# Pools of transposed x, split weights and raw weights placed first in SBUF, their tiles at multiples of 512 bytes; descriptor scratch 8 KB

## The chip, the cores and the metric

The kernel runs on one core of one Trainium2 chip. The metric is the device time of one execution in microseconds. The time before is the median of three runs.

## The reference, cut to what matters

Two blocks of two layers each act on one sequence of 256 tokens of width 1024, all in float32.

```python
# first block, per layer: mixer (attention variants), then a mixture of 16 experts
x = x + mixer(rmsnorm(x))                   # projections in, attention, projection out
x = x + ec_moe(rmsnorm(x))                  # each expert takes its 32 best tokens; silu(g) * u, down
# second block, per layer: dense ffn, mixer, dense ffn
h = h + 0.5 * swiglu(rmsnorm(h), wg, wu, wd)      # 1024 -> 2816 -> 1024
h = h + mixer(rmsnorm(h))                          # attention + convolution, or a recurrence
h = h + 0.5 * swiglu(rmsnorm(h), wg, wu, wd)
return rmsnorm(h)
```

## The kernel before, in words

The order of the work is the order of the code: the first block's even mixer (`even1`), a mixture of experts (`moe`), the odd mixer (`odd1`), a second `moe`, then in the second block `ffn`, `even2`, `ffn`, `ffn`, `odd2`, `ffn`. SyncE (SP) issues nearly all loads, in program order, on one queue.

All projections of the mixers and of the dense ffn layers work on float32 operands that are split in two parts, hi and lo, of type fp32r. `xT` writes the normed and transposed x as two tiles, `hThi` and `hTlo` (pool `hT`, 8 KB per partition each). A raw weight lands in one of six 8 KB tiles of the pool `ring`. `split` casts 1024 columns of it into a `whi` tile on ScalarE and subtracts on VectorE into a `wlo` tile (pool `wsp`, seven of each, 4 KB each). One product is then three matmuls:

```python
    def mm3(self, out, a, b, start, stop):
        mm = self.nc.tensor.matmul
        mm(out, a[0], b[0], start=start, stop=False)
        mm(out, a[0], b[1], start=False, stop=False)
        mm(out, a[1], b[0], start=False, stop=stop)
```

These are lines L406, L407 and L408. The second argument is the operand that is loaded into the array (128 columns, 512 bytes of a partition), the third one streams past it. Three uses matter here:

- Up products of the ffn (`bg`, `bu`) and the projections in of the second block (`pf`): a piece of whi or wlo is loaded, 256 columns of hThi or hTlo stream.
- Token projections of the first block (`pj`): a piece of hThi or hTlo is loaded, 512 or 256 columns of whi or wlo stream.
- Down products of the ffn and projections out (`acc`): a piece of the activations is loaded (`gh`, `gl` in the ffn's pool `fp`; `chi`, `clo` in a mixer's own pool), 512 columns of whi or wlo stream.

In an ffn layer, each of 11 steps does 96 up matmuls and the 24 down matmuls of the step before.

The `moe` stages stream expert weights that are not split: 32 loads of gate and up (two of 1 MB each) and 32 of down, into whatever is free: the ring, pairs of whi and wlo tiles (4 KB each), the two hT tiles, and up to eight extra 8 KB tiles of the pools `moew...`.

Pools take their places in SBUF in the order in which they are opened, from low to high. The DMA descriptor scratch comes first (16 KB per partition by default). In the program as built, the tiles stand at these bytes of a partition; the number behind the stroke is the remainder by 512:

| tiles | before | with the change |
|---|---|---|
| hThi, hTlo | 26560, 34752 / 448 | 8704, 16896 / 0 |
| wlo and whi, 14 tiles of 4096 | from 46240 / 160 | from 25088 / 0 |
| ring, 6 tiles of 8192 | from 103584 / 160 | from 82432 / 0 |
| x | 16512 / 128 | 131584 / 0 |
| chi, clo of even1 and odd1 | 153248, 161440 / 160 | 145440, 153632 / 32 |
| gh, gl of the first ffn; of the other three | 288; 192 | 160; 64 |
| chi, clo of even2; of odd2 | 192; 256 | 64; 128 |
| moew tiles on the right side; the others | 480; 192 | 480; 64 |

Pieces inside hT, whi, wlo, chi, clo, gh and gl start at further multiples of 512 bytes, so each piece has its tile's remainder, but for the 416, 384 and 256 column blocks of a few projections in `odd1` and `even1`.

Of the kernel before, what the change touches and what calls it, by code (L numbers as in the profile page):

```python
# [9 lines left out]
F32 = mybir.dt.float32  # L10
# [6 lines left out]
P = 128  # L17
# [10 lines left out]
RING = 6  # L28
CHUNK = 2048
PART = 1024  # L30
WB = 7
TAPS = 11
LATER = 2000
PLAN = "7ssslhrrrrrr012ssss3456" "7ssslhrrrrrrssss456"
AHEAD = 23

# [189 lines left out]
class OddLead:  # L226


    def __init__(self, A):
        self.A = A  # L230
# [53 lines left out]
class Core:  # L284
    def __init__(self, ctx, tc, A, where):
        self.tc, self.nc, self.A, self.where = tc, tc.nc, A, where
        e = ctx.enter_context
        self.cst = e(tc.tile_pool(name="cst", bufs=1))
        self.hp = e(tc.tile_pool(name="hT", bufs=1))
        self.wk = e(tc.tile_pool(name="wk", bufs=2))  # L290
        self.jk = e(tc.tile_pool(name="jk", bufs=1))
        self.ps = e(tc.tile_pool(name="ps", bufs=8, space=PSUM))
        self.n = 0
        nc = self.nc
        self.tabs = {}
        self.x = self.cst.tile([P, NT, D], F32, name="x")
        self.small("id", self.cst, nc.sync)
        self.mhalf = self.cst.tile([P, 16], F32, name="mhalf")
        nc.vector.memset(self.mhalf, -0.5)
        self.id = self.c("ident")  # L300

    def pools(self, cx, ring, parts):

        self.wp = cx.enter_context(self.tc.tile_pool(name="wsp", bufs=parts, reuse_waits="tile"))
        self.ring = cx.enter_context(self.tc.tile_pool(name="ring", bufs=ring, reuse_waits="tile"))

    def begin(self):

# [809 lines left out]
    def early(self, names):  # L1118

        for n in names:  # L1120
            self.fetch(next(i for i in range(AHEAD) if PLAN[i] == n and i not in self.got))

# [3 lines left out]
    def at(self, i):  # L1126
        return PLAN[i] if i < len(PLAN) else "r"

# [390 lines left out]
    def even2(self, nxt):  # L1519
        nc, tc, A = self.nc, self.tc, self.A  # L1520
        with ExitStack() as cx:
# [20 lines left out]
            def taps(c):  # L1542

                b = self.bank("cv")
                for j in range(31 - TAPS, 31):
                    d = pl.tile([P, P], F32, name="dgc", bufs=8)
                    nc.gpsimd.tensor_scalar(d, self.id, cw[:, c, j:j + 1], None, op0=ALU.mult)
                    nc.tensor.matmul(b[:, :S], d, glu[:, c, j:j + S], start=j == 31 - TAPS, stop=j == 30)
                with tc.high_priority(-LATER):
                    nc.vector.tensor_tensor(y[:, c], y[:, c], b[:, :S], ALU.add)  # L1550
# [14 lines left out]
            def use(i, b):  # L1565
# [15 lines left out]
                nc.vector.tensor_tensor(glu[:, c, 30:], b, sg[:, c], ALU.mult)  # L1581
                with tc.high_priority(-LATER):
                    nc.vector.tensor_scalar(y[:, c], glu[:, c, :S], cw[:, c, 0:1], cb[:, c:c + 1], op0=ALU.mult,
# [184 lines left out]
def build(tc, A, out, where):  # L1768
    with ExitStack() as ctx:
        k = Core(ctx, tc, A, where)  # L1770
        k.want(k.c("g_mix0"))
        with ExitStack() as cx:
            k.pools(cx, RING, WB)
            leads = OddLead(A), FfnLead(A)
            k.even1(k.begin(), leads[0])
            gf0 = k.cst.tile([P, KT], F32, name="gf0")
            tc.nc.vector.tensor_tensor(gf0, k.c("g_fin"), k.c("g2_f0"), ALU.mult)
            k.moe(0, (k.c("g_mix1"),), leads[0])
            k.odd1(*leads)
            k.moe(1, (gf0,), leads[1])  # L1780
            pl = cx.enter_context(tc.tile_pool(name="c2", bufs=1, reuse_waits="tile"))
            pr = cx.enter_context(tc.tile_pool(name="c2r", bufs=1, side="right", reuse_waits="tile"))
            with tc.tile_pool(name="t5", bufs=1, reuse_waits="tile") as p5:
                k.ffn(0, leads[1], (k.c("g2_m0"),), hook=k.t5_bias(pl, p5))
            k.even2((k.c("g2_f1"),))
            k.ffn(1, None, (k.c("g2_f2"),))
            k.ffn(2, None, (k.c("g2_m1"),), hook=k.log_a(pr))
            k.odd2((k.c("g2_f3"),))
            k.ffn(3, out=out)
# [17 lines left out]
```

## Time and profile before

| | |
|---|---|
| median of 3 runs (range) | 1619.71 us (1617.31 to 1621.27) |
| the profiled execution's own time | 1622.63 us |
| its span | 1620.9 us |
| TensorE busy | 1471.1 us, 91% |
| VectorE, ScalarE, GpSimd busy | 840.8, 649.4, 114.2 us |
| moved by DMA | 398.68 MB |

The span is what the profiler saw of the program's instructions; the execution's own time is 1.7 us longer. A busy time is the union of an engine's instructions.

### The profile page before, as it was taken

The page shows a single profiled execution, that of the slowest core. Times are in us where ns is not written, and L with a number is a line of the kernel's source. Part 1 is how long each engine was busy: PE and PEld are TensorE (multiplying, and loading weights), DVE is VectorE, ACT ScalarE, POOL GpSimd, SP SyncE. Part 2 cuts the span into 40 slices and gives each one's busy share as a digit, 9 for nine tenths or more (in the row PEclk, how much of TensorE's full clock was granted, in tenths as well). Part 3 has the DMA queues.
Part 4 walks back from the last instruction along what each step waited for, and adds up shares of the span by engine and source line. Part 5 has one row for each costly group of instructions (what it writes and reads, how often), then busy time and mean ns, then how long its engine had stood idle before and what let it go on. Part 6 is the DMA issues. An engine that isn't in the chain of part 4 may idle for free.

```text
span 1620.9 us, 24647 instructions
## 1 busy us (share of the span) xinstructions
PE 1471.1 (91%) x10184; PEld 1163.8 (72%) x10184; DVE 840.8 (52%) x1418; ACT 649.4 (40%) x1035; POOL 114.2 (7%) x147
## 2 busy tenths in 40 slices
PE   9998867877988677799999799999999999999998
PEld 7784204555742045599898579999999999899997
DVE  6753102258421012555569966555666559865554
ACT  5741101137311012344443544444554446754443
POOL 0000000020000001200006610000000000000000
PEclk9998979998989799899999899999999999999999
DMA  9778999992799999856454125555555553555530
GB/s 361 305 261 344 418 422 419 413 379 107 264 384 418 422 414 382 343 186 222 164 177 157 52 81 195 192 183 185 180 184 188 194 188 131 196 193 196 184 130 27
DMA packets 60625, 398.68 MB, mean 246 GB/s; under 512 B 6808, under 2 KB 7200, under 8 KB 17120
## 3 DMA queue, kind: packets, MB, share of 16 engines
q1 hardware_dynamic: 59584, 394.03, 64.3%
q0 software_dynamic: 928, 3.07, 0.6%
q8 instruction: 80, 1.31, 0.3%
q14 instruction: 33, 0.27, 0.0%
HBM read 396.01 MB, written 1.06 MB: 245 GB/s over the span
## 4 chain that ended last, share of the span: by engine, by line
PE 74%; DMA 11%; DVE 10%; ACT 4%; issue 2%; SPq 0%; POOL 0%; POOLq 0%; DVEq 0%; ACTq 0%
PE acc L406 7%; PE acc L408 7%; PE acc L407 7%; DMA w<-in_m_gu_dram 6%; PE bg L407 5%; PE bg L406 5%; PE bg L408 5%; PE bu L407 5%; PE bu L408 5%; PE bu L406 5%; DMA w<-in_m_d_dram 3%; PE by L1297 3%; DVE y L1586 3%; PE bu L1243 3%; PE bg L1243 2%; PE xs L1226 2%
## 5 line engine op out<-in xcount | busy, mean ns | idle before, releaser
L395 DVE TENSOR_TENSOR wlo<-w,whi 128x1024 fp32r<-128x1024 f32 x346 | 424.2, 1234 | 277.0 <-ACT whi L394 276.7
L394 ACT CAST whi<-w 128x1024 fp32r<-128x1024 f32 (+1 forms) x357 | 370.3, 1046 | 440.1 <-PE acc L408 143.7
L406 PE MATMUL bg<-hThi,whi 128*128 128x256 f32 x752 | 211.7, 283 | 2.8 <-ACT hThi L452 2.3
L407 PE MATMUL bg<-hTlo,whi 128*128 128x256 f32 x752 | 210.5, 281 | 3.8 <-DVE hTlo L453 3.7
L408 PE MATMUL bg<-hThi,wlo 128*128 128x256 f32 x752 | 210.6, 280 | 0.0
L407 PE MATMUL bu<-hTlo,whi 128*128 128x256 f32 x656 | 183.7, 280 | 0.0
L406 PE MATMUL bu<-hThi,whi 128*128 128x256 f32 x656 | 183.7, 280 | 0.0
L408 PE MATMUL bu<-hThi,wlo 128*128 128x256 f32 x656 | 183.6, 280 | 0.0
L407 PEld LDWEIGHTS bg<-hTlo,whi 128*128 128x128 f32 x752 | 141.8, 189 | 7.4 <-DVE hTlo L453 5.6
L406 PEld LDWEIGHTS bg<-hThi,whi 128*128 128x128 f32 x752 | 141.7, 189 | 7.0 <-ACT hThi L452 3.9
L406 PE MATMUL acc<-whi,gh 128*128 128x512 f32 x352 | 140.2, 398 | 4.9 <-ACT gh L401 4.9
L408 PEld LDWEIGHTS bg<-hThi,wlo 128*128 128x128 f32 x752 | 142.0, 189 | 0.0
L408 PE MATMUL acc<-whi,gl 128*128 128x512 f32 x352 | 140.3, 399 | 0.0
L407 PE MATMUL acc<-wlo,gh 128*128 128x512 f32 x352 | 140.3, 398 | 0.0
L406 PEld LDWEIGHTS bu<-hThi,whi 128*128 128x128 f32 x656 | 124.0, 189 | 0.0
L407 PEld LDWEIGHTS bu<-hTlo,whi 128*128 128x128 f32 x656 | 124.0, 189 | 0.0
L408 PEld LDWEIGHTS bu<-hThi,wlo 128*128 128x128 f32 x656 | 123.9, 189 | 0.0
L406 PEld LDWEIGHTS acc<-whi,gh 128*128 128x128 f32 x352 | 66.7, 189 | 19.2 <-ACT gh L401 5.1
L408 PEld LDWEIGHTS acc<-whi,gl 128*128 128x128 f32 x352 | 66.7, 189 | 16.2 <-DVE gl L402 0.6
L407 PEld LDWEIGHTS acc<-wlo,gh 128*128 128x128 f32 x352 | 66.8, 190 | 14.1
L1297 PE MATMUL by<-w,aT 128*32 128x256 f32 x1024 | 67.7, 391 | 10.0 <-DMA w<-in_m_d_dram 6.9
L1276 DVE SCALAR_TENSOR_TENSOR hid<-bu,rsl,hid 128x512 f32<-128x512 f32 x8 | 6.0, 751 | 127.4 <-PE bu L1243 119.3
(402 smaller groups left out, 2374.7 us busy)
## 6 DMA issues: line engine op xcount, KB each, us to landing
w<-in_f_gu_dram SPq DMA_DIRECT2D x84, 1024.0 KB, 5.1
w<-in_m_gu_dram SPq DMA_DIRECT2D x68, 1024.0 KB, 13.7
w<-in_m_d_dram SPq DMA_DIRECT2D x64, 1024.0 KB, 10.9
w<-in_f_d_dram SPq DMA_DIRECT2D x40, 1024.0 KB, 5.0
wx<-in_m_gu_dram SPq DMA_DIRECT2D x32, 1024.0 KB, 9.4
wx<-in_m_gu_dram SPq DMA_DIRECT2D x56, 512.0 KB, 7.0
w<-in_e_out_dram SPq DMA_DIRECT2D x8, 1024.0 KB, 4.9
w<-in_o_out_dram SPq DMA_DIRECT2D x8, 1024.0 KB, 5.1
```

Of the source, the lines that this page charges most:

```text
L394: pin(nc.scalar.copy(hi[:, i:n], w[:, o + i:o + n]))
L395: pin((eng or nc.vector).tensor_sub(lo[:, i:n], w[:, o + i:o + n], hi[:, i:n].bitcast(F32)))
L406: mm(out, a[0], b[0], start=start, stop=False)
L407: mm(out, a[0], b[1], start=False, stop=False)
L408: mm(out, a[1], b[0], start=False, stop=stop)
L1226: nc.tensor.matmul(b[:, :n], self.x[:, t, k * P:k * P + P], ohf[:, t, q0 * P:q1 * P], start=t == 0, stop=t == NT - 1)
L1243: nc.tensor.matmul(b[32 * j:32 * j + 32], xs[q][:, k, 32 * j:32 * j + 32], w[j // 2][:, j % 2 * 512:j % 2 * 512 + 512], start=k == 0, stop ...
L1276: nc.vector.scalar_tensor_tensor(a, bu, rsl[:, q:q + 1], a, op0=ALU.mult, op1=ALU.mult)
L1297: nc.tensor.matmul(b[32 * j:32 * j + 32, o:o + S], aT[:, q, f, 32 * j:32 * j + 32], w[i][:, j * S:j * S + S], start=f == 0, stop=f == 3)
L1586: nc.vector.scalar_tensor_tensor(y[:, c], glu[:, c, j:j + S], cw[:, c, j:j + 1], y[:, c], op0=ALU.mult, op1=ALU.add)
```

## The change

It opens the pools `hT`, `wsp` and `ring` first, ahead of the constants. A new pool `line` of 384 bytes (512 less the 128 that the first free byte is past a multiple) brings them to a multiple of 512; its only tile is set to zero once. The descriptor scratch goes from 16 KB to 8 KB. All tiles keep their sizes and numbers of buffers.

```diff
+LINE = 512
+SCRATCH = 8192
...
         e = ctx.enter_context
+
+        self.line(e, 128)
+        self.hp = e(tc.tile_pool(name="hT", bufs=1))
+        self.wp = e(tc.tile_pool(name="wsp", bufs=WB, reuse_waits="tile"))
+        self.ring = e(tc.tile_pool(name="ring", bufs=RING, reuse_waits="tile"))
         self.cst = e(tc.tile_pool(name="cst", bufs=1))
-        self.hp = e(tc.tile_pool(name="hT", bufs=1))
         self.wk = e(tc.tile_pool(name="wk", bufs=2))
...
-    def pools(self, cx, ring, parts):
-
-        self.wp = cx.enter_context(self.tc.tile_pool(name="wsp", bufs=parts, reuse_waits="tile"))
-        self.ring = cx.enter_context(self.tc.tile_pool(name="ring", bufs=ring, reuse_waits="tile"))
+    def line(self, e, past):
+
+        pool = e(self.tc.tile_pool(name="line", bufs=1))
+        self.tc.nc.vector.memset(pool.tile([P, (LINE - past) // 4], F32, name="line"), 0.0)
...
         with ExitStack() as cx:
-            k.pools(cx, RING, WB)
...
-    nc = _bacc.Bacc("TRN2", target_bir_lowering=False, num_devices=1)
+    nc = _bacc.Bacc("TRN2", target_bir_lowering=False, num_devices=1, dynamic_dma_scratch_size=SCRATCH)
```

The order of instructions is the same on every engine but for one new row on VectorE. Its first rows before:

```order
L299 MEMSET mhalf 128x16
L327 MEMSET warm 128x512
L499 SCALAR_TENSOR_TENSOR junk,ss<-x 128x512 x2
L453 SCALAR_TENSOR_TENSOR hTlo<-tp,pc_id,hThi 128x256 x2
L395 TENSOR_TENSOR wlo<-wz,whi 128x512
```

With the change (lines are six further down):

```order
L311 MEMSET line 128x96
L305 MEMSET mhalf 128x16
L333 MEMSET warm 128x512
L505 SCALAR_TENSOR_TENSOR junk,ss<-x 128x512 x2
L459 SCALAR_TENSOR_TENSOR hTlo<-tp,pc_id,hThi 128x256 x2
L401 TENSOR_TENSOR wlo<-wz,whi 128x512
```

The new memset of 96 columns stands ahead of the two that were first; nothing else moved.

## Rows read from the trace of the kernel before

**Rows 1.** The page: span, busy time of engines, chain that ended last by engine.
```profile
span 1620.9 us, 24647 instructions
PE 1471.1 (91%) x10184; PEld 1163.8 (72%) x10184; DVE 840.8 (52%) x1418; ACT 649.4 (40%) x1035; POOL 114.2 (7%) x147
PE 74%; DMA 11%; DVE 10%; ACT 4%; issue 2%; SPq 0%; POOL 0%; POOLq 0%; DVEq 0%; ACTq 0%
```
**Rows 2.** Stages: window, length, busy PE PEld DVE ACT POOL, clock, DMA share, GB/s.
```profile
93.10:108.40 15.30, 15.30 (x69) 12.65 (x69) 9.87 (x34) 8.86 (x22) 0.00 (x0) 1.00 0.88 338
...
185.00:340.00 155.00, 114.84 (x942) 52.19 (x935) 21.15 (x35) 18.82 (x33) 3.41 (x5) 0.90 1.01 414
500.00:570.00 70.00, 49.87 (x332) 11.89 (x328) 5.89 (x14) 3.82 (x6) 0.00 (x0) 0.79 1.01 422
...
810.00:960.00 150.00, 133.66 (x844) 115.35 (x843) 118.78 (x240) 70.94 (x126) 53.87 (x57) 0.94 0.33 113
960.00:1130.00 170.00, 169.92 (x1219) 158.58 (x1219) 99.31 (x108) 78.44 (x94) 2.52 (x6) 1.00 0.55 187
```
**Rows 3.** Groups on TensorE, whole span: line, names, shapes, count; busy us, mean ns; idle.
```profile
L406 PE MATMUL bg<-hThi,whi 128*128 128x256 f32 x752 | 211.7, 283 | 2.8 <-ACT hThi L452 2.3 <-ACT whi L394 0.4
...
L407 PE MATMUL bu<-hTlo,whi 128*128 128x256 f32 x656 | 183.7, 280 | 0.0
...
L406 PE MATMUL pf<-hThi,whi 128*128 128x256 f32 x240 | 68.0, 286 | 0.0
```
**Rows 4.** Timeline of TensorE around one ffn step: start us, length us, instruction.
```profile
1010.41 0.39 PE L406 MATMUL acc<-whi,gh 128*128 128x512 f32 x1
...
1016.01 0.28 PE L406 MATMUL bg<-hThi,whi 128*128 128x256 f32 x1
...
1027.21 0.39 PE L406 MATMUL acc<-whi,gh 128*128 128x512 f32 x1
```
**Rows 5.** Timeline of TensorE, even1's projection out, one line's first and last here.
```profile
92.69 0.39 PE L407 MATMUL acc<-wlo,chi 128*128 128x512 f32 x1
...
108.33 0.39 PE L407 MATMUL acc<-wlo,chi 128*128 128x512 f32 x1
```
**Rows 6.** Tile acc, 93 to 108.5 us: count, ns min/median/max.
```profile
L407 PE MATMUL acc<-wlo,chi x24: 389/389/389, 92.7 to 108.3; 128*128 128x512 f32 x24
```
**Rows 7.** Tile acc, 960 to 1300 us, in the ffn.
```profile
L407 PE MATMUL acc<-wlo,gh x146: 392/395/481, 993.9 to 1299.7; 128*128 128x512 f32 x146
```
**Rows 8.** Timeline of TensorE in odd1's projection out, behind a break.
```profile
431.75 0.39 PE L406 MATMUL acc<-whi,chi 128*128 128x512 f32 x1
...
432.90 0.39 PE L408 MATMUL acc<-whi,clo 128*128 128x512 f32 x1
433.13 0.39 PE L406 MATMUL acc<-whi,chi 128*128 128x512 f32 x1
...
433.81 0.39 PE L406 MATMUL acc<-whi,chi 128*128 128x512 f32 x1
```
**Rows 9.** Tile pj, whole span: count, ns min/median/max, first and last start, shapes.
```profile
L406 PE MATMUL pj<-whi,hThi x112: 277/395/775, 9.6 to 90.0; 128*128 128x512 f32 x64, 128*128 128x256 f32 x48
```
**Rows 10.** DMA packets, 510 to 570 us: rows of 8 KB.
```profile
DMA packets 3466, 25.27 MB, mean 421 GB/s; under 512 B 383, under 2 KB 383, under 8 KB 383
...
q1 hardware_dynamic: 3464, 25.24, 101.2%
```
**Rows 11.** DMA packets, 352.4 to 355.9 us: mostly rows of 4 KB.
```profile
DMA packets 363, 1.47 MB, mean 419 GB/s; under 512 B 47, under 2 KB 47, under 8 KB 321
...
q1 hardware_dynamic: 363, 1.47, 103.9%
```
**Rows 12.** Timeline of GpSimd: its largest DMA.
```profile
725.70 0.96 POOL L1649 DMA_DIRECT2D back<-t5d  x1 [2.90 <-DMA t5d<-t]
```
**Rows 13.** Tile bt: the reader of that DMA's data.
```profile
L1653 PE MATMUL bt<-back,pc_t x8: 590/592/592, 788.5 to 791.5; 128*128 128x512 f32 x8
```
**Rows 14.** Timeline of VectorE at the start.
```profile
5.53 0.69 DVE L499 SCALAR_TENSOR_TENSOR junk<-x 128x512 bf16<-128x512 f32 x1 [4.11 <-DMA x<-in_x_dram]
```

## The prediction

> **What bounds the kernel now.** I read the page first: TensorE is busy for 91% of the span and carries 74% of the chain that ended last, DMA 11%, VectorE 10% [rows 1]. [...]
>
> [...] Between 1010.41 and 1016.01 us lie the 24 down matmuls: 5.60 us / 24 = 233.3 ns each. Between 1016.01 and 1027.21 lie the 96 up matmuls: 11.20 / 96 = 116.7 ns each [rows 4]. [...]
>
> [...] In even1's projection out, matmuls of the very same shape and from the same wlo tiles run faster: line L407 starts at 92.69 and for the 24th time at 108.33 us [rows 5, 6], that is 23 x 3 matmuls in 15.64 us, 226.7 ns each, or 34/32. Their length is 389 ns for every one of the 24, while in the ffn it spreads from 392 up, with a median of 395 [rows 6, 7]. DMA moves 338 GB/s just then against 187 in the ffn [rows 2], so a quieter memory is no explanation. What differs is the table of addresses: chi and clo have the same remainder by 512 as whi and wlo (160). In the ffn gh and gl have 192 or 288, and in the up products hThi and hTlo 448 against 160. odd1's projection out, with 160 and 160, shows the same from another side: behind a break the first five follow each other in (432.90 - 431.75) / 5 = 230 ns, the next ones in (433.81 - 433.13) / 3 = 227 ns [rows 8]. I take it that the piece being loaded and the columns that stream are read side by side, and that they fall into step, after some matmuls, if their remainders are equal.
>
> **The change part by part.** *Up products.* hT, whi and wlo all get remainder 0. Their count is 3 x (752 + 656) = 4224 for the ffn and 3 x 240 = 720 for pf [rows 3]. By the code 192 of the 4224 are products that FfnLead does in the experts' stage, where DMA sets the pace; 4032 are left. The trace has no 256-column product with equal remainders. From below: nothing. [...] I take the ratio of the nearest row, 34/32: 113.3 ns, 3.4 ns less. After each 24 down products, whose remainders stay unequal, falling into step takes some 1.2 us as in rows 8, or ten of the 96; so 0.9 of 4032 x 3.4 = 12.3 us. Of pf, odd2 has 16 of 30 blocks, 384 matmuls: 1.2 us. even2's 336 lie in a stage where TensorE is busy for only 134 of 150 us and VectorE for 119 [rows 2]; I count half, 0.5 us. Sum: 14.0 us less.
>
> *Token projections.* pj has the same pair the other way round, 0 and 0 instead of 448 and 160: 3 x 64 with 512 and 3 x 48 with 256 columns [rows 9], (192 x 6.6 + 144 x 3.4) ns = 1.8 us. TensorE shares that stage's chain with the softmax on VectorE and ScalarE, so I count a third: 0.6 us less.
>
> *Projections out of even1 and odd1.* Here the equal remainders are lost (32 against 0). Each does 8 x 4 x 3 = 96 matmuls; 192 x 6.6 ns = 1.3 us more, which count nearly whole (TensorE doesn't stop in even1's, 15.30 of 15.30 us [rows 2]): 1.2 us more.
>
> *Down products.* 64 or 160 against 0 instead of 192 or 288 against 160: unequal before and after, nothing. The same for even2 and odd2.
>
> *DMA targets.* Rows of the experts' weights now start at a multiple of 512 in the ring, whi, wlo and hT; the moew tiles, 24 MB of the 192 MB, do not. What a row costs beside its bytes: 8 KB packets move 25.24 MB / (1.012 x 16 x 60 us) = 26.0 GB/s per engine, so 315 ns each [rows 10]; 4 KB packets 1.47 / (1.039 x 16 x 3.5) = 25.3, so 162 ns [rows 11]. Twice 162 less 315 leaves 9 ns per row. From above all of it could go, 2.9%, on 7/8 of the time in which DMA is full, 225 us in rows 2 and an estimated 150 around them: 9 us. From below nothing. I take nothing: tiles at remainders 160, 192 and 480 lie mixed in these stages and the rate keeps to 414 and 422 GB/s [rows 2], so it doesn't show any grading by where a row starts.
>
> [...]
>
> *The rest.* The memset of 96 columns runs while VectorE waits 4.11 us for x [rows 14]: nothing, and 0.2 us without that cover. [...] ScalarE's and VectorE's split reads ring and writes wsp with one common remainder before and after, and isn't the limit in the ffn [rows 2]: nothing.
>
> Sum: -14.0 - 0.6 + 1.2 = -13.4 us. The profiled execution took 1622.63 us, span 1620.9 and 1.7 around it, and would come to 1609.2; it lies 2.9 us over the median, which becomes 1619.71 - 13.4 = 1606.3 us.
>
> **The rivals.** *No step is found with 256 columns* (16 in 100). A load of 128 columns is half as long as the stream instead of a quarter, and the two may never settle. Then only the losses and gains of the 512-column products remain: +1.2 - 0.4, about 1620.5 us. The same follows if the remainders are not what made even1 fast. [...]
>
> *They settle into a worse step* (10 in 100), the rival on the other side. All 4700 pairs share one relation from now on, where the trace mixes several; the fixed step could be 36/32, 120 ns. It decides as soon as the common pace is over 116.7 ns: 4032 x 0.9 + 384 + 168 = 4180 matmuls x 3.3 ns = 14 us more, 1634 us. Against it: the only equal pair shown is the faster one.
>
> *DMA gains too* (12 in 100): up to 9 us beside the forecast; 1597 to 1604 us. *DMA alone gains* (4 in 100): 1611 us.
>
> *Starting on a multiple of 512 removes the whole loss* (8 in 100): 4180 x 10 ns = 42 us, 1578 us. [...]
>
> **How the numbers follow.** The forecast (50 in 100) is 1606.3 us; by itself 1601 to 1612, as the share in step runs from three quarters to all and even2's half may count whole or not at all. The range 1592 to 1622 leaves out the two far cases, 18 in 100. About 0.3%, 4.9 us, can be told from no change here. Faster by more: 50 + 12 + 4 + 8 = 74; within: 16; slower: 10.
>
> **What the profile would show.** Right: an ffn step takes 16.5 us instead of 16.80, its 96 up matmuls 10.9 instead of 11.20 with one constant length, the 24 down ones still 5.60; acc in even1 spreads from 392 ns; the experts' stages keep 414 to 422 GB/s. Wrong: up matmuls still at 116.7 ns, or a new constant over it; a rate over 425 GB/s with full DMA would move the gain to the other kind of stage.

## The result, and the profile after

The changed kernel takes 1630.56 us (median of 4 runs, 1626.93 to 1633.97), against 1620.08 for the kernel before (4 runs, 1617.31 to 1621.27): a ratio of 1.0069, 95% interval 1.0052 to 1.0086. It is slower by about 10.5 us, where 13.4 us less were forecast. The profiled execution took 1633.97 us. One run of E1 below took 2008.84 us at a mean granted clock of 0.68, where all others had 0.95 to 0.97; the times given leave it out.

The head of the page answers to [rows 1]: TensorE's busy time grew by 12.4 us, about as much as the span, 11.3.

```profile
span 1632.2 us, 24646 instructions
PE 1483.5 (91%) x10184; PEld 1176.8 (72%) x10184; DVE 841.5 (52%) x1419; ACT 648.5 (40%) x1035; POOL 114.0 (7%) x147
PE 75%; DVE 10%; DMA 10%; ACT 3%; issue 2%; SPq 0%; POOL 0%; POOLq 0%; DVEq 0%; ACTq 0%
```

The table of stages, with the columns of [rows 2], shows a change in two kinds of stage. In the dense ffn TensorE is as busy as before and does 1197 matmuls in the time of 1219. In the experts' stages DMA now reaches 427 GB/s in one window; in the other it moves 414 as before, with a share of 0.99 instead of 1.01.

```profile
185.00:340.00 155.00, 114.80 (x956) 52.84 (x946) 22.27 (x39) 18.89 (x33) 3.40 (x5) 0.91 0.99 414
500.00:570.00 70.00, 50.53 (x328) 12.44 (x324) 6.38 (x15) 3.32 (x6) 0.00 (x0) 0.78 1.01 427
...
960.00:1130.00 170.00, 169.92 (x1197) 158.67 (x1196) 97.42 (x105) 75.65 (x92) 2.50 (x6) 1.00 0.55 185
```

Where the time comes in shows in the first and last start of two tiles: the experts' down product `by`, whose last start ends the first block, and the ffn's first line of `acc`, whose last start is near the end. First of before, then of the changed kernel (count, ns min/median/max, first and last start).

```profile
L1297 PE MATMUL by<-w,aT x1024: 379/379/637, 247.0 to 658.4; 128*32 128x256 f32 x171
L406 PE MATMUL acc<-whi,gh x352: 390/395/795, 678.8 to 1612.4; 128*128 128x512 f32 x176
```

```profile
L1303 PE MATMUL by<-w,aT x1024: 378/379/636, 245.4 to 656.1; 128*32 128x256 f32 x171
L412 PE MATMUL acc<-whi,gh x352: 388/394/794, 676.6 to 1623.7; 128*128 128x512 f32 x176
```

Up to the end of the experts the changed kernel is 658.4 - 656.1 = 2.3 us ahead. From there to the end it takes 1623.7 - 656.1 = 967.6 us instead of 1612.4 - 658.4 = 954.0: 13.6 us lost. 13.6 - 2.3 is the 11.3 us between the spans.

Of the two, only the loss repeats from trace to trace. The stretch from the one last start to the other takes 952.6 us in E1 and 952.8 in E7 below, whose up products stand as far apart as before, and 966.2 in E2, where they stand as in the changed kernel. The last start of `by`, though, lies anywhere from 647.0 to 658.4 us in the fifteen profiled executions, and from 651.4 to 658.4 in the four whose weights all land off multiples of 256 bytes (before, E2, E7, E9). So one pair of traces doesn't measure a lead of 2.3 us.

The timeline of one ffn step answers to [rows 4].

```profile
1012.67 0.40 PE L412 MATMUL acc<-whi,gh 128*128 128x512 f32 x1
...
1018.27 0.28 PE L412 MATMUL bg<-hThi,whi 128*128 128x256 f32 x1
...
1029.77 0.40 PE L412 MATMUL acc<-whi,gh 128*128 128x512 f32 x1
```

The 24 down matmuls take 5.60 us as before. The 96 up matmuls take 11.50 instead of 11.20, so a step 17.10 instead of 16.80, and 44 steps cost 13.2 us: nearly the whole loss. Worked out from the starts in the trace, the first eight or so of each 96 vary, and the rest follow each other in 120.0 ns; before, the mean of the 96 was 116.7 (11.20 us / 96).

The tile `bg` in the ffn of the second block, for weight loads (PEld) and matmuls, first of before and then of the changed kernel, says which instruction grew:

```profile
L406 PEld LDWEIGHTS bg<-hThi,whi x96: 187/188/189, 1021.5 to 1119.2; 128*128 128x128 f32 x96
L406 PE MATMUL bg<-hThi,whi x96: 277/280/281, 1021.6 to 1119.3; 128*128 128x256 f32 x96
```

```profile
L412 PEld LDWEIGHTS bg<-hThi,whi x107: 187/192/192, 1019.9 to 1129.0; 128*128 128x128 f32 x107
L412 PE MATMUL bg<-hThi,whi x107: 277/283/283, 1020.0 to 1129.1; 128*128 128x256 f32 x107
```

A load that took 187 to 189 ns takes 192 once the pace has settled, and the matmul beside it 283 instead of 277 to 281. Nothing waits in between; the groups over the whole span, which answer to [rows 3], show the same 3 to 4 ns:

```profile
L412 PE MATMUL bg<-hThi,whi 128*128 128x256 f32 x752 | 213.8, 286 | 2.7 <-ACT hThi L458 2.3 <-ACT whi L400 0.4
L413 PE MATMUL bu<-hTlo,whi 128*128 128x256 f32 x656 | 185.9, 283 | 0.0
L412 PE MATMUL pf<-hThi,whi 128*128 128x256 f32 x240 | 68.8, 290 | 0.0
```

even1's projection out, the 1st and the 24th start of its second line and the tile, against [rows 5, 6]:

```profile
91.38 0.39 PE L413 MATMUL acc<-wlo,chi 128*128 128x512 f32 x1
...
107.48 0.40 PE L413 MATMUL acc<-wlo,chi 128*128 128x512 f32 x1
```

16.10 us / 69 = 233.3 ns instead of 226.7: this product lost its equal remainders and its pace.

DMA packets from 510 to 570 us, against [rows 10]: 25.59 MB in 1.010 x 16 x 60 us, 26.4 GB/s for each engine instead of 26.0. In the packets' records nearly all 8 KB rows of this window take 309 ns; before, they lay from 309 to 322. Their mean is 309.3 instead of 314.1 ns, and this repeats: 314.0 to 314.1 in E2, E7 and E9, whose rows start at 160 too, and 309.3 to 309.6 in all other kernels below but E5, whose ring has mixed starts.

```profile
DMA packets 3512, 25.62 MB, mean 427 GB/s; under 512 B 387, under 2 KB 387, under 8 KB 387
...
q1 hardware_dynamic: 3510, 25.59, 101.0%
```

VectorE's start, against [rows 14]: the new memset ends long before x is there.

```profile
0.82 0.14 DVE L311 MEMSET line<- 128x96 f32 x1 [0.82 <-PEq L1801]
...
5.15 0.69 DVE L505 SCALAR_TENSOR_TENSOR junk<-x 128x512 bf16<-128x512 f32 x1 [3.63 <-DMA x<-in_x_dram]
```

### The profile page after: what moved, and what is told of

Same layout as the page of the kernel before. It is cut to its first block, busy times and chain, and to the rows that moved or that the text cites. A ratio compares the mean times of both kernels' runs of the same rounds, so it can differ in the third digit from the quotient of the medians.

```text
span 1632.2 us, 24646 instructions
## 1 busy us (share of the span) xinstructions
PE 1483.5 (91%) x10184; PEld 1176.8 (72%) x10184; DVE 841.5 (52%) x1419; ACT 648.5 (40%) x1035; POOL 114.0 (7%) x147
## 4 chain that ended last, share of the span: by engine, by line
PE 75%; DVE 10%; DMA 10%; ACT 3%; issue 2%; SPq 0%; POOL 0%; POOLq 0%; DVEq 0%; ACTq 0%
PE acc L412 7%; PE acc L413 7%; PE acc L414 7%; DMA w<-in_m_gu_dram 6%; PE bg L413 5%; PE bg L412 5%; PE bg L414 5%; PE bu L413 5%; PE bu L414 5%; PE bu L412 5%; PE by L1303 3%; DMA w<-in_m_d_dram 3%; PE bu L1249 3%; DVE y L1592 3%; PE bg L1249 2%; PE xs L1232 2%
## 5 line engine op out<-in xcount | busy, mean ns | idle before, releaser
L414 PE MATMUL pf<-hThi,wlo 128*128 128x256 f32 x240 | 68.2, 286 | 2.2 <-DVE wlo L401 2.2
## 6 DMA issues: line engine op xcount, KB each, us to landing
w<-in_m_gu_dram SPq DMA_DIRECT2D x68, 1024.0 KB, 13.4
```

## The experiments

Below, the distance of a product is where the streamed columns begin less where the loaded piece begins, by 512 bytes. Theory A: the distance sets the pace of fp32r matmuls. Theory B: a start on a multiple of 512 is itself slow. The 36/32 of theory A under E1 stands for the 120.0 ns of the changed kernel. All kernels issue the same instructions in the same order but for what a diff shows. Times of before are those measured beside each group of runs.

**E1: hT 288 bytes further.** The changed kernel with hT read at remainder 288 (`HOFF` is 288 for each use), so that the up products have the distance of before. The experts' weights still land at the start of the hT tiles.

```diff
-                self.hT = (self.hp.tile([P, KT, S], F32R, tag="hThi", name="hThi"),
-                           self.hp.tile([P, KT, S], F32R, tag="hTlo", name="hTlo"))
+                o = HOFF[self.nh] // 4
+                self.nh += 1
+                self.hT = [self.hp.tile([P, KT * S + 128], F32R, tag=n, name=n)[:, o:o + KT * S]
+                           .rearrange("p (k s) -> p k s", k=KT) for n in ("hThi", "hTlo")]
```

> The changed kernel with one thing altered: hThi and hTlo begin 288 bytes behind a multiple of 512 where TensorE reads them; split and raw weights stay at remainder 0, and so do the experts' weights that land in the hT tiles. The up products' two operands then stand 288 bytes apart by 512, as in the kernel before. Theory A (the distance between the streamed columns and the piece being loaded sets the pace; equal remainders lock into 36/32): up matmuls back at a mean of 116.7 ns, an ffn step at 16.8 us; the 44 steps give back 0.3 us each and the time comes to 1616 to 1618 us, a little under the kernel before, by the 2.4 us that the DMA part brought. Theory B (a start on a multiple of 512 is itself slow to read, for instance for the split weights against other traffic): up matmuls stay near 120 ns, as the loaded pieces still start on multiples of 512, and the time stays at 1628 us or more.

1614.87 us beside 1618.69 of before, ratio 0.9979 (0.9965 to 0.9993). One step in its timeline:

```profile
1007.49 0.39 PE L413 MATMUL acc<-whi,gh 128*128 128x512 f32 x1
...
1013.08 0.28 PE L413 MATMUL bg<-hThi,whi 128*128 128x256 f32 x1
...
1024.28 0.39 PE L413 MATMUL acc<-whi,gh 128*128 128x512 f32 x1
```

The up matmuls are back at 11.20 us for 96, with the loaded pieces still at multiples of 512. Theory B falls. What is left of the change is a small gain, by the ratio 3.4 us (1.1 to 5.7).

**E2: everything 160 bytes further.**

```diff
-        self.line(e, 128)
+        self.line(e, 128 - 160)
```

> The changed kernel with everything on the left side of memory moved up by 160 bytes: hT, split and raw weights all have remainder 160, every distance between two operands is the same as in the changed kernel, and no row lands on a multiple of 512. Theory A (distance alone): up matmuls still 120.0 ns, an ffn step 17.1 us; packets of 8 KB spread again from 309 to 322 ns with a mean near 314, the experts' stages lose what they gained, and the time is 1631 to 1635 us. Theory B (multiples of 512 are slow): up matmuls at 116.7 ns or below, 1617 to 1621 us.

1632.82 us, ratio 1.0092 (1.0066 to 1.0119). The tile `bg` and the DMA packets from 510 to 570 us:

```profile
L412 PEld LDWEIGHTS bg<-hThi,whi x92: 187/192/192, 1019.9 to 1112.2; 128*128 128x128 f32 x92
L412 PE MATMUL bg<-hThi,whi x92: 277/283/283, 1020.0 to 1112.3; 128*128 128x256 f32 x92
```

```profile
DMA packets 3474, 25.29 MB, mean 422 GB/s; under 512 B 389, under 2 KB 389, under 8 KB 389
...
q1 hardware_dynamic: 3472, 25.26, 101.2%
```

No tile stands on a multiple of 512, and the up matmuls still take 120.0 ns: distance 0 is enough. DMA is back at 422 GB/s, so its gain in rate did come from where rows land. (The times don't show that part by themselves: the intervals of E2 and of the changed kernel overlap.) With E1 this parts the change in two: the distance made the loss; the landing places made the faster rows, and with them, most likely, the small gain.

**E3: eight distances in one run.** E1's code with another list.

```diff
+HOFF = [64, 128, 32, 288, 128, 256, 64, 384]
```

> The changed kernel with another distance of hT in each of its eight uses: even1 64, odd1 128, first ffn 32, even2 288, second ffn 128, third ffn 256, odd2 64, last ffn 384 bytes, with the split weights at 0. One look, read by the pace of the up matmuls in each stage. Theory A: each distance has a pace of its own, between 113 and 120 ns; 256 is the fastest, near 113 ns (30 lone pairs 256 apart in the kernel before took 113.0), 32 is near the bad end. Theory B: all stages at 120 ns, since the loaded pieces are at 0 in all of them. A third theory, that only equal remainders lock and all others are alike: 116 to 117 ns in all stages.

1618.33 us in one run. The distances do differ (the table under E5 has their paces), so theory B and the third theory fall, but 256 is no good one: its ffn has the same rows as distance 0.

```profile
L413 PEld LDWEIGHTS bg<-hThi,whi x112: 187/192/193, 1182.7 to 1299.2; 128*128 128x128 f32 x112
L413 PE MATMUL bg<-hThi,whi x112: 277/283/284, 1182.8 to 1299.3; 128*128 128x256 f32 x112
```

The expectation of 113 ns rested on 30 lone pairs at the border of up and down products; their pace did not carry over to a lasting one, 119.8 ns.

**E4: down products with equal remainders.** As E1, with gh and gl at remainder 0.

```diff
-            half = pl.tile([P, NT], F32, name="half", bufs=1)
+            half = pl.tile([P, NT + (448 - 96 * (i == 0)) // 4], F32, name="half", bufs=1)[:, :NT]
```

> As the kernel with hT at 288, and gh and gl of the ffn layers moved to remainder 0 as well, so that the down products' loaded pieces and streamed columns have equal remainders, with 512 columns. Theory A: the down matmuls go from 233.4 to between 229 and 227 ns as in the projections out with equal remainders before, an ffn step from 16.8 to 16.65 to 16.7 us, and the time is 4 to 7 us under that of the kernel with hT at 288: 1610 to 1613 us. Theory C (equal remainders are bad with any count of columns, and even1's fast projection out had another cause): down matmuls at or over 233.4 ns, no gain or a loss.

1609.35 us, ratio 0.9952 (0.9938 to 0.9966). One step:

```profile
1017.91 0.39 PE L413 MATMUL acc<-whi,gh 128*128 128x512 f32 x1
...
1023.38 0.28 PE L413 MATMUL bg<-hThi,whi 128*128 128x256 f32 x1
```

24 down matmuls in 5.47 us instead of 5.60; 44 steps x 0.13 = 5.7 us, and 5.5 were measured against E1. With 512 columns equal remainders are good (5.47 us / 24 = 227.9 ns instead of 233.3), with 256 they are bad (120.0 ns instead of 116.7 at 288).

**E5: eight more distances, and a ring with six remainders.** E3's code with `HOFF = [192, 320, 448, 480, 192, 160, 416, 96]`, and 64 bytes more for each ring tile.

```diff
-            t = self.ring.tile([P, CHUNK], F32, tag="ring", name="w")
+            t = self.ring.tile([P, CHUNK + RPAD], F32, tag="ring", name="w")[:, :CHUNK]
```

> The changed kernel with further distances of hT in its eight uses: even1 192, odd1 320, first ffn 448, even2 480, second ffn 192, third ffn 160, odd2 416, last ffn 96 bytes; and the six ring tiles 64 bytes longer, so that they begin at remainders 0, 64, 128, 192, 256 and 320. One look. The scan before gave 119.8 ns for 0 and 256, 116.8 for 32 and 288, 119.2 for 128 and 384, 117.8 for 64: pairs half a row of 512 apart agree. If the pace repeats with 256 bytes, 448 and 192 agree here, and so do 160 and 416; the token projections at 448 took 114.9, so the first and second ffn should be the fastest seen, 113 to 115 ns. If it doesn't repeat, 448 and 192 differ by over 0.5 ns. For DMA: tiles of the ring at 0 land 2.43 us behind one another in full stretches. If only multiples of 512 are free of the extra cost, the five others take 2.47 to 2.50; if multiples of 256 are, the one at 256 takes 2.43 too; if multiples of 64 are, all do (against it: experts' tiles at 64 took 2.48 in the changed kernel).

1611.56 us in one run. The second ffn, at 192, one step and its tile:

```profile
1021.59 0.28 PE L414 MATMUL bg<-hThi,whi 128*128 128x256 f32 x1
...
1032.49 0.39 PE L414 MATMUL acc<-whi,gh 128*128 128x512 f32 x1
```

```profile
L414 PEld LDWEIGHTS bg<-hThi,whi x120: 187/188/188, 1010.5 to 1127.7; 128*128 128x128 f32 x120
L414 PE MATMUL bg<-hThi,whi x120: 276/276/285, 1010.7 to 1127.8; 128*128 128x256 f32 x120
```

10.90 us for 96; loads at 188 and matmuls at 276 ns. Means over all pairs that follow each other without a gap, worked out from the starts in the traces of before, the changed kernel, E1 to E5 and E13:

| columns | distance: ns from start to start |
|---|---|
| 256, up and pf | 0: 119.8; 16: 117.1; 32: 116.8; 64: 117.8; 96: 119.9; 128: 119.2; 160: 118.6; 176: 119.2; 192: 113.6 here; 208: 118.8; 240: 117.2; 256: 119.8; 288: 116.8; 384: 119.2; 416: 117.7; 448: 113.7; 480: 118.3 |
| 512, acc and pj | 0: 227 to 229; 64: 229.0; 320: 229.1; 192, 224, 384, 448, 480: 232 to 233.4; 96, 352: 233.4; 416: 234.2 |

With 256 columns every distance but 0, 192 and 288 was seen in one execution only. Places half of 512 apart mostly agree (0 and 256, 32 and 288, 128 and 384, 192 and 448; 160 and 416 are 0.9 ns apart). For DMA, where a load's tile is worked out from the order of the loads, since the trace has no addresses, the median gap between landings of 1 MB in full stretches was 2.44 us for ring tiles at 0 and 256 and 2.475 to 2.483 at 64, 192 and 320; the tile at 128 took 2.49 in the first `moe` and 2.45 in the second, which stays unexplained. In the kernel before, with all six at 160, it was 2.484.

**E6: the projections out too.** As E4, with chi and clo of all mixers at remainder 0.

```diff
-            chi = h0.tile([P, KT, S], F32R, name="chi")
+            chi = h0.tile([P, KT * S + 120], F32R, name="chi")[:, 120:].rearrange("p (k s) -> p k s", k=KT)
```

That is for even1 and odd1; in even2 and odd2 the pads are 112 and 96 columns.

> As the kernel with hT at 288 and gh, gl at 0, and chi and clo of the four mixers at remainder 0 too: every product with 512 columns has equal remainders, the up products are 288 apart. Four projections out of 96 matmuls each should go from 233 to 227 to 229 ns: at most 384 x 6 ns = 2.3 us, of which even1's and odd1's count nearly whole and even2's and odd2's in part. Theory A: 1607 to 1608.5 us, 0 to 2.3 under the 1609.35 of the kernel without it. Theory C (the projections out are limited by the split of the weights): no difference, 1609 to 1610.

1610.63 us, ratio 0.9946 (0.9927 to 0.9965). All 512-column pairs with distance 0 now average 227.7 ns, but the time can't be told from E4's: the 2 us are below what the runs resolve, so this stays inconclusive.

**E7: the scratch alone**, in the kernel before.

```diff
-    nc = _bacc.Bacc("TRN2", target_bir_lowering=False, num_devices=1)
+    nc = _bacc.Bacc("TRN2", target_bir_lowering=False, num_devices=1, dynamic_dma_scratch_size=8192)
```

> The kernel before with the scratch of the dynamic DMAs set to 8 KB and nothing else; all tiles move down by 8192 bytes and keep their remainders. Every theory expects no change, 1618 to 1620 us, 0.998 to 1.002 of before; a rival that descriptor writes have to wait in half the room would show GpSimd's DMA issues longer than 0.96 us and a slower even2.

1619.56 us, ratio 1.0002 (0.9987 to 1.0018): nothing. GpSimd's largest DMA is issued in 0.96 us as in [rows 12].

```profile
724.01 0.96 POOL L1649 DMA_DIRECT2D back<-t5d  x1 [3.02 <-DMA t5d<-t]
```

**E8: hT at 192, down products equal.** As E4, with hT at 192 in all its uses.

```diff
-                self.hT = (self.hp.tile([P, KT, S], F32R, tag="hThi", name="hThi"),
-                           self.hp.tile([P, KT, S], F32R, tag="hTlo", name="hTlo"))
+                self.hT = [self.hp.tile([P, KT * S + 128], F32R, tag=n, name=n)[:, 48:48 + KT * S]
+                           .rearrange("p (k s) -> p k s", k=KT) for n in ("hThi", "hTlo")]
```

> As the kernel with hT at 288 and gh, gl at 0, but hT at 192, the distance with which the two scans had up matmuls of 113.6 ns. Theory A: some 4,600 up matmuls (those of the ffn and two thirds of pf) by 116.8 - 113.6 = 3.2 ns, 14.5 us under the 1609.35 us of that kernel: 1593 to 1597 us; an ffn step at 96 x 113.6 + 24 x 228 = 16.4 us, TensorE still without a gap in the ffn. Rival: another bound stands close behind (the split of the weights on ScalarE and VectorE, or the loads), and the time stops at 1600 us or above with TensorE waiting in the ffn.

1612.18 us, ratio 0.9961 (0.9945 to 0.9976): a miss by 15 us. TensorE had no gaps in the ffn (busy for 339.85 of the 340 us from 960 on), so the rival of a bound behind it falls as well. The tile:

```profile
L412 PEld LDWEIGHTS bg<-hThi,whi x110: 187/188/188, 1020.1 to 1128.0; 128*128 128x128 f32 x110
L412 PE MATMUL bg<-hThi,whi x111: 281/281/281, 1019.9 to 1128.1; 128*128 128x256 f32 x111
...
L414 PEld LDWEIGHTS bg<-hThi,wlo x111: 192/192/192, 1020.0 to 1128.3; 128*128 128x128 f32 x111
```

It is the distance of E5's second ffn, but another lasting pace: one load of three takes 192 ns, without exception, and the starts follow in 117, 118, 118 instead of 113, 113, 114. A step's 96 up matmuls take 11.31 us.

**E9: only hT moved, in the kernel before.** hT at 352, 192 from the split weights at 160; scratch at 8 KB for the room.

```diff
-                self.hT = (self.hp.tile([P, KT, S], F32R, tag="hThi", name="hThi"),
-                           self.hp.tile([P, KT, S], F32R, tag="hTlo", name="hTlo"))
+                self.hT = [self.hp.tile([P, KT * S + 128], F32R, tag=n, name=n)[:, 104:104 + KT * S]
+                           .rearrange("p (k s) -> p k s", k=KT) for n in ("hThi", "hTlo")]
```

> The kernel before, with hT alone moved so that it stands 192 bytes from the split weights (hT at 352, split and raw weights still at 160, all in the order of before; scratch at 8 KB, which by itself changed nothing, for the room). Theory A: the distance is all that counts for TensorE, so the up matmuls take 113.6 ns without any tile at a multiple of 512: some 14.5 us off 1619, 1603 to 1606 us, with 8 KB packets still at a mean near 314 ns. Rival: the pace at 192 needs the loaded pieces at remainder 0 (as they were in both scans): up matmuls stay at 116 to 117 ns and the time at 1617 to 1620 us.

1607.36 us, ratio 0.9930 (0.9906 to 0.9954).

```profile
1016.89 0.39 PE L406 MATMUL acc<-whi,gh 128*128 128x512 f32 x1
...
1022.48 0.28 PE L406 MATMUL bg<-hThi,whi 128*128 128x256 f32 x1
...
1033.37 0.39 PE L406 MATMUL acc<-whi,gh 128*128 128x512 f32 x1
```

10.89 us for 96 up matmuls, with no remainder altered but hT's and no tile of hT, `wsp` or the ring at a multiple of 512: the lowest median of all kernels timed more than once comes from a distance alone (it can't be told from those of E10 and E11 below, whose intervals overlap with this one). From the last start of `by` to the last of `acc` it takes 943.5 us instead of 954.0, so the trace puts 10.5 us of the gain there; the 8 KB packets keep a mean of 314.1 ns. The time lies 1.4 us over what was expected; the first two full steps of each of the last three layers ran at 11.31 to 11.39.

**E10: hT at 192, gh and gl at 448.** As E8, with the distances of E5's second ffn in all four layers.

```diff
-            half = pl.tile([P, NT + (448 - 96 * (i == 0)) // 4], F32, name="half", bufs=1)[:, :NT]
+            half = pl.tile([P, NT + (384 - 96 * (i == 0)) // 4], F32, name="half", bufs=1)[:, :NT]
```

> As the kernel with hT at 192 and gh, gl at 0, but gh and gl of all four ffn layers at 448, so that the down products' two operands stand 64 bytes apart by 512. In the second scan this pair of distances had down matmuls of 229 ns and up matmuls that reached 113, 113, 114 after six and stayed there; with gh at 0 the same distance of the up products stayed at 117, 118, 118. Theory A2 (distance 192 has two lasting states, and the spacing that the down products leave decides which one a step falls into): an ffn step at 10.90 + 5.49 = 16.4 us against 11.31 + 5.44 = 16.75; 44 steps x 0.35 = 15 us under the kernel with gh at 0, 1595 to 1600 us. Rival (gh at 0 had nothing to do with it, the state is drawn anew in each execution): up matmuls at 117.8 ns in part of the steps, 1600 to 1612 us, with a wide spread between runs.

1609.11 us, ratio 0.9939 (0.9925 to 0.9952), 9 us or more above what theory A2 expected. In the profiled execution nearly all steps of the first ffn took 10.9 us for their up matmuls and those of the other three 11.31, with the same distances: theory A2, that gh's place decides, falls, and the rival's picture, 117.8 ns in part of the steps, fits.

**E11: the changed kernel with hT at 192 alone.** E8's edit of hT, and gh and gl left at 160 and 64:

```diff
+                self.hT = [self.hp.tile([P, KT * S + 128], F32R, tag=n, name=n)[:, 48:48 + KT * S]
+                           .rearrange("p (k s) -> p k s", k=KT) for n in ("hThi", "hTlo")]
```

> The changed kernel with hT alone moved to 192 bytes behind a multiple of 512; gh and gl stay at 160 and 64, so the down products' distances are those of the changed kernel. Theory A2 with the lasting state reached from down products of unequal remainders, as in the kernel before with hT moved alone: an ffn step at 10.9 + 5.6 = 16.5 us against 17.1, 44 x 0.6 = 26 us under the changed kernel, 1602 to 1606 us. Rival: the slower state, 11.31 + 5.6 = 16.9 us a step, 1620 to 1623 us.

1607.94 us, ratio 0.9937 (0.9922 to 0.9951), between the two expectations. From the second ffn on, steps of 10.90 and 11.31 us alternate, one by one: with these distances each pace leads into the other.

**E12: E10 once more, with no edit.**

> The kernel with hT at 192 and gh, gl at 448 once more, unaltered, for a second profile of it. In the first, the nine steps of the first ffn took 10.9 us for their 96 up matmuls and the thirty of the other three 11.31, with the same distances. If the layout and the order fix the state, the same steps come out at 10.9 and 11.31 again and the time is near 1613; if the state is drawn anew by small shifts of timing, other layers are in the fast state, and the time lies 12.6 us x (their share of the thirty steps) lower.

1606.74 us in one run, on another chip than E10's; 6.6 less than the profiled execution of E10. One step of the second ffn, in E10 and then here:

```profile
1023.99 0.28 PE L412 MATMUL bg<-hThi,whi 128*128 128x256 f32 x1
...
1035.30 0.40 PE L412 MATMUL acc<-whi,gh 128*128 128x512 f32 x1
```

```profile
1023.47 0.28 PE L412 MATMUL bg<-hThi,whi 128*128 128x256 f32 x1
...
1034.38 0.39 PE L412 MATMUL acc<-whi,gh 128*128 128x512 f32 x1
```

11.31 against 10.91 us, in one and the same program. Here the second and the last ffn kept the lower pace and the third the higher one. So at this distance program and addresses don't fix the pace of a layer. It is kept within a layer here, but not in E9 and E11. As the two profiles come from two chips, it is not shown that the pace also changes between executions on one chip; E10's six runs on one chip spread over 6.5 us, which would fit.

**E13: distances of 16 bytes.** E3's code with `HOFF = [0, 0, 176, 208, 208, 240, 16, 16]`.

> The changed kernel with distances of hT that are multiples of 16 bytes only: first ffn 176, even2 208, second ffn 208, third ffn 240, odd2 and last ffn 16; even1 and odd1 at 0. One look at the pace of the up matmuls. If a distance near 192 is what keeps stream and load apart, 176 and 208 are at 113.5 to 115 ns; if the pattern repeats with a unit of 32 or 64 bytes and 16 counts for nothing, 16 is at 120 like 0 and 208 at 113.6 or 117.8 like 192; 240 lies between 224 (118.3) and 0 (120).

1620.49 us in one run; the paces stand in the table under E5. 176 and 208 are at 119.2 and 118.8, so in this run the low pace of 192 did not reach 16 bytes to either side.

## Why the prediction was wrong, point by point

- *The bound* was read rightly: in the ffn TensorE is busy for 169.92 of 170 us before and after, with full DMA the rate is 414 to 427 GB/s, and all that changed is how fast matmuls follow each other (120.0 ns instead of 116.7) and how fast bytes land (309.3 ns for an 8 KB row instead of 314.1).
- *Up products, -14.0 us.* This is the step that failed: "I take the ratio of the nearest row, 34/32: 113.3 ns". No run shows the whole of which 34/32 is a share; the traces show 226.7 against 233.3 ns, and 116.7 x 226.7 / 233.3 comes to the same 113.4 ns. The nearest row had 512 columns. With 256, equal remainders settle at 120.0 ns (E2 shows the distance as the cause, E1 the way back). That they settle, and after some ten matmuls, was right, and so was the count: 44 steps x 0.30 = 13.2 us and a little of pf make the 13.6 measured. The rival "they settle into a worse step" described this and gave 14 us; its chance was put at 10 in 100 because "the only equal pair shown is the faster one", which was one pair with another number of columns. Of its own signs of being wrong, "a new constant over it" is what the rows show.
- *Token projections, -0.6 us.* With 512 columns they went from 233.3 to 227.4 ns on the mean, as the ratio said. With 256 columns they got slower, from a median of 117 to one of 120 ns, as the up products did, so the 1.8 us before the third were 192 x 5.9 - 144 x 3 ns = 0.7 us. Neither can be told from the scatter of that stage.
- *Projections out, +1.2 us.* Right in kind and size: 233.3 ns in even1 instead of 226.7, 96 x 6.6 ns = 0.6 us for each.
- *Down products, nothing.* Right, 5.60 us before and after. E4 shows what lay there: 5.5 us for pads of 352 and 448 bytes.
- *DMA targets, taken as nothing.* Mis-sized: an 8 KB row takes 309.3 ns instead of 314.1, and E1, with the distance of before in the up products, is 3.4 us faster than before (1.1 to 5.7), inside the bounds of 0 to 9. The reason given was that the rate didn't grade by where a row starts. But before, all tiles in those stages stood at 160, 192, 448 or 480, and these cost alike (medians of 2.484 us per MB in the ring at 160 and 2.485 in the other 8 KB tiles); the contrast that would have shown it, a start at 0 or 256, was not in the trace. E5 has it: 2.44 us at 0 and 256 against 2.475 to 2.483 at 64, 192 and 320, these three within 0.01 us of each other.
- *Memset and split*: nothing, as said. The scratch was worth nothing either: E7's ratio is 1.0002, and GpSimd's largest DMA, which before is issued in 0.96 us at 725.70 and first read at 788.5 [rows 12, 13], is issued in 0.96 us there too.
- *Read side by side* was the author's estimate; no run shows how the two operands are read. E1 and E2 show that the distance of the streamed and the loaded piece sets the pace: a step takes 16.80 or 17.10 us by it, and the load itself is what grows, from 188 to 192 ns.
- *The rival of a whole loss removed* counted 10 ns for each of 4180 matmuls, which no run shows: the lowest mean pace with 256 columns was 113.6 ns (E5), 3.1 under the 116.7 of before.

In sum: -14.0 became about +13.5, 0 became a gain of a few us, and the remaining terms, 1.2 us at most, are below what the runs resolve.

What stays open is why the pace depends on the distance as it does, with 256 columns and 512 columns at odds, and what picks one of the two paces at 192. The runs show the pace and the length of the loads, not the memory behind them.

## What to carry to other kernels

Where matmuls run back to back with a load before each, measure their pace from start to start for each shape and ask how far apart the streamed and the loaded tile stand by 512 bytes: here a pad of 416 bytes in front of each of hT's two tiles was worth 12 us (E9; 7.4 to 15.2 by its interval), and making everything a round multiple cost 10. Don't carry such a ratio from one number of columns to another; scan the distances, several in one run, and profile the winner twice, as a lasting pace can differ between two executions of one program (E10 and E12, on two chips). Landing places at remainder 0 or 256 made rows land 1.5 to 2% faster where DMA was full (309.3 ns instead of 314.1 for 8 KB in the changed kernel; 2.44 us instead of 2.475 to 2.483 for 1 MB in E5), and that can be had without equal remainders of the operands (E1).

## What the runs showed of the hardware that was not expected

- fp32r matmuls of one shape, with no wait between them, ran at mean paces from 113.6 ns (E5, distance 192) to 119.9 (E5, 96) with 256 columns and from 226.7 ns (even1 before, 0) to 234.2 (odd2 before, 416) with 512, by the distance of their two operands' places.
- Distance 0 gave nearly the slowest pace seen with 256 columns (119.8 ns; the slowest was 119.9) and the fastest with 512 (227 to 229 ns, where the slowest was 234.2).
- At distance 192 there are two paces, 10.90 and 11.31 us for 96 matmuls, and each can last for a whole layer (E12). In the higher one, exactly every third weight load takes 192 ns instead of 188 (E8); at distance 0, all do but the first few of a step (the changed kernel).
- With DMA full, 1 MB landed in 2.44 us where rows start at 0 or 256 by 512 (E5) and in 2.475 to 2.484 us at 64, 192 and 320 (E5) and 160 (before); a tile at 128 took 2.49 in one `moe` and 2.45 in the other (E5). A packet of 8 KB took 309.3 to 309.6 ns on the mean in kernels with rows at 0, and 314.0 to 314.1 in those with rows at 160.
